# Memory tokens first, two weight parts in buffers of their own, and the second half of x normalised sooner, in a one-core hybrid encoder trunk

## The chip, the cores and the metric

The kernel runs on one core of one Trainium2 chip. The metric is the device time of one execution in microseconds (us), smaller being better. The engines are named as the profile names them: PE is TensorE's matmul side and PEld its weight loads, DVE is VectorE, ACT is ScalarE, POOL is GpSimd, and SP (queue SPq) is the engine that issues every DMA here.

## What is computed

One layer of a streaming encoder, on x of 1024 positions by 1024 features, all in float32:

```
h    = layer_norm(x, ln_in_g, ln_in_b)
proj = h @ w_in + b_in                       # 3912 columns, split among four head groups
ya   = spatial_gating(gelu(a_u), gelu(a_v))  # group A
yb   = chunk_band_attention(bq, bk, bv)      # group B
yc   = dsa_attention(cq, ck, cv, iq, ik, iw) # group C: indexer scores, top 256 keys, attention
km, vm = split(mem @ w_mem_kv, 2)            # 256 memory tokens, 512 columns
ym   = memory_attention(mq, km, vm)          # group M
mixed = concat(ya*silu(a_g), yb*silu(bg), yc*silu(cg), ym*silu(mg))
out  = layer_norm(2**0.25 * h + mixed @ w_out + b_out, ln_g, ln_b)
```

The change lies in the opening: the input norm of x, the product `mem @ w_mem_kv`, and the first columns of `proj` (the indexer's key `ik` and the gate `mg`).

## The kernel before

**Precision.** Every float32 product is made of three passes: each operand is split into a rounded high part and the rest, and high by high, high by rest and rest by high are added up in PSUM (`project`, L211). A block of 128 weight columns is loaded by `wblock` (L193) as a tile `raw` (two buffers, tag `raw`). For each half of its rows ACT writes the high part and POOL subtracts it for the rest (L206, L207). The two halves go into tiles of tag `w`, of which there are five (`WB`).

**The opening, in program order.** `FIRST_LOADS` (L48) gives the order of the first loads: x is a block of 128 rows of x (512 KB), g is the norm's gain broadcast to all partitions, m is half of the memory tokens (512 KB), w is one 128-column block of `w_mem_kv` (512 KB). Then come the norm's shift as columns and the projection's bias (`load_biases`, L145, three loads of single elements by column). `mem_parts` (L319) turns the memory tokens on PE and splits them into `mT` (ACT the high part, DVE the rest). `x_rows` (L289) normalises one block of x: DVE takes the statistics in two pieces, aggregates them, POOL makes the reciprocal root (L133, L134), DVE subtracts and multiplies, ACT scales. `kv_of_mem` (L373) makes the keys (i = 0) and then the values (i = 1) of the memory tokens, 24 matmuls of 256 columns for each of four weight blocks. The third and fourth blocks are loaded inside its first call (L380), into the two `raw` buffers of the first two, so each of these loads waits until POOL has read its predecessor. `x_parts` (L303) turns four normalised blocks of x on PE, 32 transposes for half of the sequence, and splits them into `hTh` (ACT) and `hTl` (DVE). After that come two more weight blocks, `wik` (L388, 72 columns) and `wmg` (L389), again in the `raw` buffers. `ik_half` and `gate_half` (L394, L336) project each half of the sequence with them, 24 matmuls each.

**What holds the second half of x.** Blocks 4 to 7 of x go into tiles of their own tags (`s4`, `score7`, `v3`, `v3`, L284). Two explicit orders stand on them:

```
    with tc.issue_after(loads[3]):
        xts += [x_load(rb) for rb in range(4, NB)]
    ik_half(0, 512)
    with tc.issue_after(first_half[0]):
        for rb in range(4, NB):
            x_rows(rb, xts[rb])
```

The first makes SP issue the four x loads behind the fourth block of `w_mem_kv` (`loads[3]`). The second puts the DVE work of `x_rows` for blocks 4 to 7 behind the last `hTl` of the first half (`first_half[0]` is a DVE instruction).

**Who sets the order.** Each engine runs its instructions in a fixed order. That order is made when the program is built: a planner goes through a simulated time and gives each engine the ready instruction that stands first in the program (some, under `high_priority`, are moved forward). So a change in the opening can move instructions of later stages too. SP serves its DMA issues in its own fixed order. Nearly all operations are recorded under one helper line, L93, so the trace is read by tiles. Behind the opening stand the indexer's queries and scores, the gates of A, then attention groups M, B and C woven with projections and a top-k search on DVE and ACT, then the output projection and the last norm.

Of the kernel before, what the change touches and what calls it, by code (L numbers as in the profile page):

```python
# [11 lines left out]
F32 = mybir.dt.float32  # L12
# [12 lines left out]
P = 128  # L25
NB = 8
KT = 8
# [11 lines left out]

C0_FIRST, LATE = (0, 1, 6, 7, 5), "17 16 15 14 04 13 03 12 02 11 10"  # L40
HR = 2
WH = (0, 0)
MHB = 2
LAG_O = 14
OB, LB = 400, 0
LG_AT = 0
PRELOAD = (6,)
FIRST_LOADS = "xgmxmwxwx"  # L48
ML_V = (6,)
HR_V = 6  # L50
LB_V = (7, 6)
# [21 lines left out]
def f32(ap):  # L73
    return ap.bitcast(F32)
# [3 lines left out]
def tile_trunk(ctx, tc, x, mem, ln_in_g, ln_in_b, w_in, b_in, a_ln_g, a_ln_b, a_ws, a_bs,  # L78
               b_rel_rev, t5_table, w_mem, w_out, b_out, ln_g, ln_b, bucket1h, out):
    nc = tc.nc  # L80
    G, SP = nc.gpsimd, nc.sync
# [22 lines left out]
    def run(steps):  # L104

        while True:
            try:
                next(steps)
            except StopIteration as e:
                return e.value  # L110

    cp = ctx.enter_context(tc.tile_pool(name="cp", bufs=1))
    gp = ctx.enter_context(tc.tile_pool(name="gp", bufs=1))
# [13 lines left out]
    def bcast(t, vec):  # L127
        n = vec.shape[-1]
        SP.dma_start(out=t, in_=bass.AP(tensor=vec.tensor, offset=vec.offset, ap=[[0, P], [1, n]]))
# [39 lines left out]
    def s4(name, dt=F32R, shape=(P, SEQ)):  # L169
        return gp.tile(list(shape), dt, tag="s4", bufs=S4, name=name)  # L170
# [11 lines left out]
    E = ep.enter_context(tc.tile_pool(name="ep", bufs=1))  # L182

    def ev(name, bufs=EV):
        return E.tile([P, 512], F32, tag="ev", bufs=bufs, name=name)
# [4 lines left out]

    loads = []

    def wblock(w, c0, m=P):  # L193

        raw = E.tile([P, KT, P], F32, tag="raw", bufs=2, name="raw")
        loads.append(SP.dma_start(out=raw[:, :, :m], in_=w[:, c0:c0 + m].rearrange("(k p) c -> p k c", p=P)).ins)
        ts = []
        if m < P:
            narrow = [gp.tile([P, 2, KT // 2, m], F32R, tag=tag, bufs=1, name="wnar") for tag in ("planes", "score6")]
        for q in range(2):  # L200
            t = E.tile([P, 2, 4, P], F32R, tag="w", bufs=WB, name="wblk") if m == P else narrow[q]
            r = raw[:, 4 * q:4 * q + 4, :m]
            if WH[0] <= len(loads) < WH[1]:
                G.tensor_scalar(t[:, 0], r, 1.0, 0.0, ALU.mult, ALU.add)
            else:
                S.activation(t[:, 0], r, AF.Copy)  # L206
            G.tensor_sub(t[:, 1], r, f32(t[:, 0]))  # L207
            ts.append(t)
        return ts

    def project(t, a, b, m=P, hi=hh, lo=hl, tag="pp"):  # L211

        acc = bank(tag, "acc")
        for k in range(KT):
            wh, wl = t[k // 4][:, 0, k % 4, :m], t[k // 4][:, 1, k % 4, :m]
            PE.matmul(acc[:m, :b - a], wh, hi(k, a, b), start=(k == 0), stop=False)
            PE.matmul(acc[:m, :b - a], wh, lo(k, a, b), start=False, stop=False)
            PE.matmul(acc[:m, :b - a], wl, hi(k, a, b), start=False, stop=(k == KT - 1))
            yield
        return acc  # L220
# [62 lines left out]
    def x_load(rb):  # L283
        tag = ("S", "S", "S", "S", "s4", "score7", "v3", "v3")[rb]  # L284
        xt = gp.tile([P, DM], F32, tag=tag, bufs={"S": SB, "v3": 2, "s4": S4}.get(tag, 1), name="xt")
        SP.dma_start(out=xt, in_=x[rb * P:(rb + 1) * P, :])
        return xt

    def x_rows(rb, xt):  # L289

        st = E.tile([P, 2, 6], F32, tag="st", bufs=2, name="st")
        V.bn_stats(st[:, 0], xt[:, :512])
        V.bn_stats(st[:, 1], xt[:, 512:])
        mv = E.tile([P, 2], F32, tag="mv", bufs=2, name="mv")
        V.bn_aggr(mv, st)
        rs = E.tile([P, 1], F32, tag="rs", bufs=2, name="rs")
        with tc.high_priority(offset=BOOST):
            rstd_of(mv[:, 1:2], rs)
        V.scalar_tensor_tensor(xt, xt, mv[:, 0:1], g_in, ALU.subtract, ALU.mult)
        with tc.high_priority(offset=BOOST):  # L300
            S.activation(xt, xt, AF.Copy, scale=rs)

    def x_parts(half, xts):  # L303

        high, rest = hT[half]
        for k in range(KT):
            pt = bank(("pt", "qk")[k % 2], "xT")
            for j in range(4):
                PE.transpose(pt[:, j * P:(j + 1) * P], xts[j][:, k * P:(k + 1) * P], ident)
            begin = S.activation(high[:, k, :], pt, AF.Identity, bias=b_col[:, k:k + 1])  # L310
            end = V.scalar_tensor_tensor(rest[:, k, :], pt, b_col[:, k:k + 1], f32(high[:, k, :]), ALU.add, ALU.subtract)
        return end.ins, begin.ins
# [44 lines left out]
    xts, mts, w_kv = [], [], []  # L357
    for what in FIRST_LOADS:
        if what == "x":
            xts.append(x_load(len(xts)))  # L360
        if what == "m":
            mts.append(mem_load(len(mts)))
        if what == "w":
            w_kv.append(wblock(w_mem, len(w_kv) * P))
        if what == "g":
            bcast(g_in, ln_in_g)
# [6 lines left out]
    def kv_of_mem(i):  # L373

        t = ev("kv")
        for pair in range(2):
            acc = run(project(w_kv[2 * i + pair], 0, 256, P, mhi, mlo))
            S.activation(t[:, pair * 256:pair * 256 + 256], acc[:, :256], AF.Copy)
            if not i:
                w_kv.append(wblock(w_mem, 256 + pair * P))  # L380
        return t

    km = kv_of_mem(0)
    first_half = x_parts(0, xts)
    vm = kv_of_mem(1)


    wik = wblock(w_in, I_K, 72)  # L388
    wmg = wblock(w_in, M_G)  # L389
    ikh = s4("ikh")  # L390
# [3 lines left out]
    def ik_half(a, b):  # L394
        acc = run(project(wik, a, b, 72))
        bk = col[I_K]
        with tc.high_priority(offset=BOOST):
            for lo in (0, 64):
                S.activation(ikh[lo:lo + 64, a:b], acc[0:64, :], AF.Identity, bias=bias[0:64, bk:bk + 1])
            S.activation(iwT[64:72, a:b], acc[64:72, :], AF.Identity, bias=bias[64:72, bk:bk + 1])  # L400
            for lo in (0, 64):
                V.scalar_tensor_tensor(ikl[lo:lo + 64, a:b], acc[0:64, :], bias[0:64, bk:bk + 1],
                                       f32(ikh[0:64, a:b]), ALU.add, ALU.subtract)

    with tc.issue_after(loads[3]):
        xts += [x_load(rb) for rb in range(4, NB)]
    ik_half(0, 512)
    with tc.issue_after(first_half[0]):
        for rb in range(4, NB):
            x_rows(rb, xts[rb])  # L410
    run(gate_half(wmg, M_G, 6, 0, "pv"))
    second_half = x_parts(1, xts[4:])
# [375 lines left out]
    for g in range(4):  # L788
        SP.dma_start(out=bsT[64 * (g % 2):64 * (g % 2) + 64, g // 2, :],
                     in_=bass.AP(tensor=a_bs.tensor, offset=a_bs.offset + g * P, ap=[[0, 64], [1, P]]))  # L790
# [438 lines left out]
    def hr_load(rb):  # L1229
        hr = L.tile([P, DM], F32, tag="hr", bufs=HR, name="hr") if rb > HR_S4 else s4("hr", F32)  # L1230
        SP.dma_start(out=hr, in_=h_dram[rb])
        return hr
# [69 lines left out]
    for k in range(KT):  # L1302
        hi, lo = [t[:, k % 4, :] for t in wo[k // 4]]
        raw = E.tile([P, DM], F32, tag="raw", bufs=2, name="rawo")
        SP.dma_start(out=raw, in_=w_out[k * P:(k + 1) * P, :])
        for half in range(2):
            c = slice(half * 512, half * 512 + 512)
# [11 lines left out]
    bcast(bo, b_out)  # L1319
    shift = L.tile([P, DM], F32, tag="hr", bufs=HR, name="shift")  # L1320
    bcast(shift, ln_in_b)
# [59 lines left out]
```

## Time and profile before

| what | value |
|---|---|
| median of 3 runs | 681.34 us (678.85 to 681.65) |
| the profiled execution's own time | 681.43 us |
| its span, first to last instruction | 679.6 us |
| PE busy | 642.8 us, 95% of the span |
| DVE busy | 493.5 us, 73% |
| ACT busy | 421.6 us, 62% |
| POOL busy | 342.2 us, 50% |
| mean granted TensorE clock | 0.984 of full speed |

A busy share is a mean over stages with different limits. PE's 95% says that the time is PE's work and 5% of gaps; what the change can win is in those gaps, and the question is where they lie. Times in the rows are us from the span's start. In brackets behind an instruction stands how long its engine was idle before it, and what released it.

### The profile page before, as it was taken

The numbers are of one execution on the slowest core, as the hardware profiler recorded it, in microseconds if no ns is written. First come the engines' busy times: TensorE is split into PE (matmuls) and PEld (weight loads), VectorE is DVE, ScalarE is ACT, GpSimd is POOL, SyncE is SP. The second block draws the span as 40 slices with busy tenths as digits, with TensorE's granted clock in tenths as the row PEclk, the third lists the DMA queues.
The fourth block names the chain that finished last, engine by engine and source line by source line (L and its number), as shares of the span: only waits on it lengthen the run. The fifth ranks groups of instructions, "written<-read, shape, count | busy, mean of one in ns | idle before, by whom it ended". The sixth has DMA issues, their size and how long they took to land. (4 is left out here: it accounts for less than half of the span.)

```text
span 679.6 us, 11076 instructions
## 1 busy us (share of the span) xinstructions
PE 642.8 (95%) x3698; PEld 486.7 (72%) x3698; DVE 493.5 (73%) x1183; ACT 421.6 (62%) x937; POOL 342.2 (50%) x346
## 2 busy tenths in 40 slices
PE   4889999899999999979999999999998999999995
PEld 3857876677787777757667767667776777777785
DVE  6585256557867899899897888976668688687635
ACT  4665255447599998685898896545545664555310
POOL 3682321105436786483577245983222634559741
PEclk9999999899999999997999999999999999999998
DMA  9793511012234544455467524564102383234111
GB/s 279 235 306 100 169 51 32 1 47 67 73 109 100 108 119 114 90 123 141 82 136 137 101 75 102 115 115 120 35 16 95 126 265 106 89 108 158 63 62 63
DMA packets 121669, 75.30 MB, mean 111 GB/s; under 512 B 58976, under 2 KB 111500, under 8 KB 121612
## 3 DMA queue, kind: packets, MB, share of 16 engines
q1 hardware_dynamic: 121612, 74.59, 40.5%
q8 instruction: 29, 0.48, 0.3%
q14 instruction: 28, 0.23, 0.1%
HBM read 46.44 MB, written 17.64 MB: 94 GB/s over the span
## 5 line engine op out<-in xcount | busy, mean ns | idle before, releaser
L93 PE MATMUL acc<-hTh,wblk 128*128 128x512 f32 (+1 forms) x960 | 322.6, 404 | 4.7 <-DVE iql L93 2.6
L93 PEld LDWEIGHTS acc<-hTh,wblk 128*128 128x128 f32 x960 | 179.0, 191 | 52.8 <-issue 8.2
L93 PE MATMUL acc<-hTl,wblk 128*128 128x512 f32 (+1 forms) x480 | 190.4, 397 | 0.0
L207 POOL TENSOR_TENSOR wblk<-raw,wblk 128x512 fp32r<-128x512 f32 x72 | 101.0, 1407 | 124.3 <-ACT wblk L93 119.0
L93 ACT ACTIVATE jka<-score,cand 128x768 int8<-128x768 f32 (+2 forms) x93 | 96.4, 1037 | 14.8 <-DVE cand L93 14.1
L93 PEld LDWEIGHTS acc<-hTl,wblk 128*128 128x128 f32 x480 | 91.5, 191 | 19.3 <-issue 2.6
L93 PEld LDWEIGHTS <-pT 128*128 128x128 f16 x656 | 45.7, 99 | 32.5 <-issue 25.2
L93 DVE SCALAR_TENSOR_TENSOR score<-relu,iw,score 128x384 f32<-128x384 f32 (+5 forms) x42 | 43.7, 1059 | 23.9 <-ACT relu L93 22.1
L545 POOL TENSOR_TENSOR sc<-sc 128x512 f16<-128x512 f32 (+4 forms) x48 | 58.0, 1213 | 2.3
L93 ACT ACTIVATE wblk<-raw 128x512 fp32r<-128x512 f32 x72 | 44.5, 627 | 23.3 <-PE acc L93 13.5
L93 PE MATMUL acc<-woh,mh 128*128 128x512 f32 (+1 forms) x144 | 55.6, 387 | 0.0
L93 PE MATMUL pv<-v,pT 128*128 128x192 bf16 (+1 forms) x528 | 53.9, 234 | 0.8 <-DMA pT<-sc 0.8
L93 PE MATMUL acc<-wol,mh 128*128 128x512 f32 (+1 forms) x144 | 54.3, 377 | 0.0
L93 PE MATMUL acc<-woh,ml 128*128 128x512 f32 (+1 forms) x144 | 53.7, 374 | 0.4 <-DVE ml L93 0.4
L93 ACT ACTIVATE relu<-qk 128x384 f32<-128x384 f32 (+2 forms) x80 | 35.9, 530 | 24.1 <-PE qk L93 23.7
L544 POOL TENSOR_SCALAR sc<-sc 128x512 f16<-128x512 f32 (+4 forms) x48 | 31.2, 652 | 34.8 <-ACT sc L93 32.8
L93 ACT ACTIVATE sc<-sc,nb 128x640 f32<-128x640 f32 (+7 forms) x64 | 46.5, 729 | 1.4
L93 ACT ACTIVATE pT<-pt 128x512 f16<-128x512 f32 (+3 forms) x48 | 22.3, 484 | 36.1 <-PE pt L93 35.9
L93 DVE TENSOR_SCALAR_CACHE_REDUCE jk<-planes,lo 128x384 bf16<-128x384 uint16 (+2 forms) x48 | 35.7, 744 | 1.2
L93 ACT ACTIVATE o<-o,ri 128x64 f32<-128x64 f32 x96 | 27.9, 340 | 12.4 <-DVE o L93 12.2
L93 PE MATMUL qk<-kh,qh 64*128 64x384 f32 (+3 forms) x96 | 32.7, 417 | 1.9 <-DVE mx L93 1.7
L93 DVE TENSOR_SCALAR_CACHE_REDUCE jk<-planes,cand 128x384 bf16<-128x384 bf16 (+2 forms) x45 | 33.5, 744 | 1.1
(205 smaller groups left out, 1235.1 us busy)
## 6 DMA issues: line engine op xcount, KB each, us to landing
raw<-in_w_in SPq DMA_DIRECT2D x32, 512.0 KB, 3.8
xt<-in_x SPq DMA_DIRECT2D x8, 512.0 KB, 4.8
h_dram<-xt SPq DMA_DIRECT2D x8, 512.0 KB, 5.8
gate<-t SPq DMA_DIRECT2D x16, 256.0 KB, 2.1
rawo<-in_w_out SPq DMA_DIRECT2D x8, 512.0 KB, 4.1
hr<-h_dram SPq DMA_DIRECT2D x8, 512.0 KB, 4.4
out<-hr SPq DMA_DIRECT2D x7, 512.0 KB, 2.6
gate<-gate SPq DMA_DIRECT2D x48, 64.0 KB, 2.0
```

Source lines behind the costliest of these rows:

```text
L93: ins = op(*a, **k)
L207: G.tensor_sub(t[:, 1], r, f32(t[:, 0]))
L544: G.tensor_scalar(high, sc[:, :n], 1.0, 0.0, ALU.mult, ALU.add)
L545: G.tensor_sub(rest, sc[:, :n], high)
```

## The change

The first loads take the order mem, mem, w, x, g, x, w, x, x in place of x, g, mem, x, mem, w, x, w, x. The third and fourth blocks of `w_mem_kv` are loaded outside `kv_of_mem`, each in two halves of 256 KB, into tiles of the tags `jk`, `vt` and `near`, which nothing else uses until much later. The loads of x's blocks 4 to 7 follow them in the program, before the memory's keys, with no order put on them. The DVE work of blocks 4 and 5 is no longer held behind the first half's last `hTl`; that of blocks 6 and 7 still is.

```
+X_FREE = 5
-FIRST_LOADS = "xgmxmwxwx"
+FIRST_LOADS = "mmwxgxwxx"

-    def wblock(w, c0, m=P):
-
-        raw = E.tile([P, KT, P], F32, tag="raw", bufs=2, name="raw")
-        loads.append(SP.dma_start(out=raw[:, :, :m], in_=w[:, c0:c0 + m].rearrange("(k p) c -> p k c", p=P)).ins)
+    def wblock(w, c0, m=P, places=None):
+
+        src = w[:, c0:c0 + m].rearrange("(k p) c -> p k c", p=P)
+        if places:
+            raws = [gp.tile([P, 4, P], F32, tag=tag, bufs=bufs, name="raw") for tag, bufs in places]
+            for q in range(2):
+                loads.append(SP.dma_start(out=raws[q], in_=src[:, 4 * q:4 * q + 4]).ins)
+        else:
+            raw = E.tile([P, KT, P], F32, tag="raw", bufs=2, name="raw")
+            loads.append(SP.dma_start(out=raw[:, :, :m], in_=src).ins)
+            raws = [raw[:, 4 * q:4 * q + 4, :m] for q in range(2)]
...
-            r = raw[:, 4 * q:4 * q + 4, :m]
+            r = raws[q]
...
             acc = run(project(w_kv[2 * i + pair], 0, 256, P, mhi, mlo))
             S.activation(t[:, pair * 256:pair * 256 + 256], acc[:, :256], AF.Copy)
-            if not i:
-                w_kv.append(wblock(w_mem, 256 + pair * P))
         return t
 
+    for pair in range(2):
+        w_kv.append(wblock(w_mem, 256 + pair * P, places=((("jk", 1), ("vt", 1)), (("near", 2), ("near", 2)))[pair]))
+    xts += [x_load(rb) for rb in range(4, NB)]
     km = kv_of_mem(0)
     first_half = x_parts(0, xts)
     vm = kv_of_mem(1)
...
-    with tc.issue_after(loads[3]):
-        xts += [x_load(rb) for rb in range(4, NB)]
     ik_half(0, 512)
-    with tc.issue_after(first_half[0]):
-        for rb in range(4, NB):
+    for rb in range(4, NB):
+        with tc.issue_after(first_half[0]) if rb > X_FREE else ExitStack():
             x_rows(rb, xts[rb])
```

## Rows read from the trace of the kernel before

**Rows 1.** Windows of 40 us: PE, PEld, DVE, ACT, POOL busy, clock, DMA share, GB/s.

```profile
0.00:40.00 40.00, 28.52 (x174) 24.41 (x174) 26.59 (x65) 21.06 (x36) 23.53 (x29) 0.96 0.83 247
40.00:80.00 40.00, 36.43 (x199) 28.59 (x198) 19.85 (x32) 21.97 (x35) 15.02 (x15) 1.00 0.63 209
...
280.00:320.00 40.00, 34.27 (x198) 26.55 (x197) 37.69 (x99) 27.55 (x69) 23.04 (x32) 0.91 0.42 106
```

**Rows 2.** Windows of 5 us in the opening, the same columns.

```profile
10.00:15.00 5.00, 3.42 (x14) 2.25 (x12) 4.96 (x9) 3.84 (x7) 3.08 (x3) 1.00 1.10 383
15.00:20.00 5.00, 4.89 (x29) 4.89 (x29) 4.93 (x10) 1.03 (x2) 5.00 (x6) 0.66 0.86 79
20.00:25.00 5.00, 5.00 (x44) 4.97 (x43) 0.31 (x1) 3.89 (x6) 4.74 (x5) 1.00 0.55 172
...
45.00:50.00 5.00, 2.90 (x23) 2.19 (x21) 2.27 (x4) 3.88 (x6) 1.98 (x4) 1.00 1.02 341
```

**Rows 3.** Timeline of PE in the opening: start, duration, instruction, idle before.

```profile
7.99 1.94 PE L93 MATMUL pt<-ident,mt 128*128 128x128 f32 x8 [7.99 <-DMA mt<-in_mem]
...
17.58 2.39 PE L93 MATMUL acc<-mT,wblk 128*128 128x256 f32 x11
...
22.15 3.16 PE L93 MATMUL acc<-mT,wblk 128*128 128x256 f32 x24
...
33.27 0.46 PE L93 MATMUL acc<-hTh,wnar 128*72 128x512 f32 x1 [1.48 <-ACT wnar L93]
...
44.90 1.25 PE L93 MATMUL xT<-ident,xt 128*128 128x128 f32 x10
...
47.54 0.77 PE L93 MATMUL xT<-ident,xt 128*128 128x128 f32 x5 [1.39 <-ACT xt L93]
```

**Rows 4.** Timeline of SP's DMA issues, from the fourth x block on.

```profile
7.45 2.99 SPq L286 DMA_DIRECT2D xt<-in_x  x1
...
10.96 5.89 SPq L149 DMA_DIRECT2D bias<-in_b_in  x3
...
17.51 4.36 SPq L196 DMA_DIRECT2D raw<-in_w_mem_kv  x2
21.92 2.01 SPq L286 DMA_DIRECT2D xt<-in_x  x4
24.85 10.42 SPq L196 DMA_DIRECT2D raw<-in_w_in  x3
```

**Rows 5.** DMA issues to landing: all x (median), x at 0.72 and 7.45, wik.

```profile
xt<-in_x SPq DMA_DIRECT2D x8, 512.0 KB, 4.8
...
xt<-in_x SPq DMA_DIRECT2D x1, 512.0 KB, 3.4
...
xt<-in_x SPq DMA_DIRECT2D x1, 512.0 KB, 8.6
...
raw<-in_w_in SPq DMA_DIRECT2D x1, 288.0 KB, 7.9
```

**Rows 6.** Timeline of DVE: last row block of the first half, hTl, second half.

```profile
19.02 1.28 DVE L93 SCALAR_TENSOR_TENSOR xt<-xt,mv,g_in 128x1024 f32<-128x1024 f32 x1
27.31 4.04 DVE L93 SCALAR_TENSOR_TENSOR hTl<-xT,b_col,hTh 128x512 fp32r<-128x512 f32 x6 [7.01 <-ACT hTh L93]
...
33.39 2.46 DVE L93 BATCH_NORM_STATS2 st<-xt 128x6 f32<-128x512 f32 x4
...
41.13 4.45 DVE L93 SCALAR_TENSOR_TENSOR xt<-xt,mv,g_in 128x1024 f32<-128x1024 f32 x2
```

**Rows 7.** Timeline of ACT around the first half's high parts.

```profile
25.55 1.15 ACT L93 ACTIVATE wblk<-raw 128x512 fp32r<-128x512 f32 x2 [1.56 <-DMA raw<-in_w_mem_kv]
26.61 2.98 ACT L93 ACTIVATE hTh<-xT,b_col 128x512 fp32r<-128x512 f32 x5
```

**Rows 8.** Instructions on the tile raw to 60 us: ns least, median, most.

```profile
L93 ACT ACTIVATE wblk<-raw x14: 615/620/632, 12.1 to 58.6; 128x512 fp32r<-128x512 f32 x14
L207 POOL TENSOR_TENSOR wblk<-raw,wblk x14: 1277/1296/2342, 13.8 to 59.3; 128x512 fp32r<-128x512 f32 x14
```

## The prediction, made before the changed kernel ran

> **What bounds the kernel now.** I read the busy table first: PE is busy for 642.8 of 679.6 us, so only a gap of PE, or slow clock under PE, can be won. The windows then say where the gaps lie. PE is idle for 11.48 us of the first 40 and 3.57 us of the next 40 [rows 1], which is 15.05 of its 36.8 us of gaps; the stage from 280 to 320 us, far from the change, has another 5.73. In finer windows the opening has two more faces [rows 2]: from 15 to 20 us PE runs at a mean granted clock of 0.66 (a stretch at the lower level, 1.2 GHz), and from 45 to 50 us it is idle for 2.10 us.
>
> The PE timeline names what it waits for [rows 3]. Its first work, the turning of the memory tokens, starts at 7.99 us, released by their DMA. The indexer's key `ik`, the first product that needs x, starts at 33.27, released by ACT's conversion of `wik`. At 44.90 the work on the first half ends and PE turns the second half of x, where it waits for ACT's scaling of late blocks (1.39 us before 47.54).
>
> SP and the DMA views give the cause of 33.27. Two loads of w_mem parts go out in the 4.36 us from 17.51, the second only once POOL has freed a `raw` buffer; the x loads follow at 21.92 and `wik` at 24.85, behind another buffer [rows 4], to land 7.9 us later [rows 5], at 32.75. Meanwhile the DMA engines moved only 172 GB/s from 20 to 25 us, against 383 from 10 to 15 [rows 2]. ACT too stood for 1.56 us for the fourth part, with the first `hTh` queued behind it at 26.61 [rows 7]. DVE ended the first half's rows at 19.02 + 1.28 = 20.30 and then idled 7.01 us [rows 6]. The second half's rows, held behind the last `hTl`, filled it from 33.39 to 41.13 + 4.45 = 45.58, which is 12.2 us for four blocks, 3.05 each.
>
> **The change, part by part.**
>
> *First loads.* The first load of the queue lands 3.4 us after its issue at 0.72 [rows 5]. It is now mem, so PE's first transposes start near 4.1 and not at 7.99. The last of the nine still lands at 7.45 + 8.6 = 16.05, since the bytes are the same. x's first block, first before, is now fourth: at 383 GB/s a load of 0.52 MB takes 1.37 us, so three of them put it near 8.3. DVE then has four blocks, each with two statistics (2.46 us for four), a small aggregate and a multiply of 1.28 [rows 6], which I estimate at 2.8 us; 8.3 + 11.2 is 19.5, so it ends near 20 as before. By itself this buys PE early work and no early x: I count 0 for it, and it is the cover that lets the keys of the first two blocks be over by about 18, where PE was still at them at 22.15 [rows 3].
>
> *Parts three and four, in their own tiles.* The two waits for POOL in SP's queue go. The biases stand ahead as before: SP is busy on them to 10.96 + 5.89 = 16.85 [rows 4], and from 15 to 20 us the DMA engines are 0.86 busy at 79 GB/s [rows 2], so nothing large moves before about 19. From there w_mem parts (1.05 MB), x blocks 4 to 7 (2.10) and `wik` (0.29) are 3.44 MB, 9.0 us at 383 GB/s: `wik` lands between 28 and 29.3. With its ACT conversion PE could start `ik` at 28.8 to 30. Is PE free by then? The fourth part lands near 22 to 23, ACT takes 2 x 0.62, POOL 2 x 1.30 [rows 8], then 24 matmuls of 0.132 (3.16 us for 24) [rows 3]: 23 + 1.2 + 2.6 + 3.2 = 30.0. `hTh` no longer stands behind a late weight on ACT and starts near 22, eight at 0.6 [rows 7], so `hTl` ends near 28. I take `ik` at 30.0: **3.3 us sooner** than 33.27. Bounds: 0, if something else holds it to 33.3, and 4.5 at 28.8. The two extra DMA issues cost SP about 0.4 us each by the spacing of the four x issues (2.01 for four gives 0.5) [rows 4]; the data takes 9 us from 19, so the issues lie under it; uncovered they would cost 1 us.
>
> *Blocks 4 and 5 set free.* They land near 23 to 25 and can fill DVE between and around the `hTl` work (8 x 0.67 us from 4.04 for six [rows 6]). From 22: 5.4 for `hTl`, four blocks at 3.05, 1.5 for `ikl`, is 19.1: the last block leaves DVE near 41 instead of 45.58. PE needs it when its first-half work ends, 44.90 - 3.3 = 41.6, and ACT's scale lies between (1.15 us, as for two weight halves of the same size together [rows 7]), so most of the wait is gone. The gaps of 3.57 us between 40 and 80 us [rows 1] lie mostly here; I take **2.0 us** of them, with bounds 0 and 3.5. SP is passed by these loads too: the stores of x that follow wait for ACT's scaling and only come sooner.
>
> *POOL beside DVE.* More DVE work now lies beside POOL's weight subtraction. These two slow each other: the subtraction took 1.296 us at the median and 2.342 at the most [rows 8], DVE's multiply 1.28 alone and 2.22 each in the pair from 41.13 [rows 6]. One such hit on the path is 1.05; I take **0.5 lost**, bounds 0 and 2.1.
>
> *Clock.* Eleven key matmuls took 2.39 us in the slow stretch and 24 took 3.16 in the fast one [rows 3], 0.217 against 0.132. The stretch from 15 to 20 costs 0.34 x 5 = 1.7 us. It began after PE had worked on and off, with 3.42 of 5 us busy from 10 to 15 [rows 2]. The new opening has such a stretch somewhere as well: 0, bounds -1.7 (it falls where PE waits anyway) and +1.7 (a second one).
>
> *The rest.* The planner orders all engines anew. I see no reason for a sign: 0, with 2 us to either side, since single gaps such as those in the stage at 280 us [rows 1] can grow or shrink by that.
>
> Sum against the profiled execution, 681.43 us (span 679.6 and 1.8 around it, 0.09 over the median of 681.34): 681.43 - 3.3 - 2.0 + 0.5 = 676.6.
>
> **The rivals.** *Slower: x blocks in DVE's way.* Blocks 4 and 5 now may stand ahead of `hTl` in DVE's fixed order. If the planner puts both there and they land as late as before (issue at 21.92 [rows 4], 4.8 at the median [rows 5]), DVE is held to 26.7 + 2 x 3.05 = 32.8, against 27.31 for the first `hTl` now. `hTl` frees the PSUM banks of x's transposes, of which five are there for eight, so three rounds of transposes stay behind it and `ik` starts at about 35.5 (+2.3); blocks 6 and 7 follow `hTl` and give no gain either; a slow-clock stretch adds 1.7: 685.4. It decides if the first `hTl` comes after 29.5. Against it: block 4 should land at 23 to 24, as no buffer holds its load, and then the pair costs only DVE's idle time.
>
> *No change: one term only.* The parts of w_mem wait behind the biases anyway, and ACT must do all of the late blocks, `hTh`, and four conversions between 20 and 30. If this holds `ik` to 32 or later, only 1.3 and half of the second term are left: 681.43 - 1.3 - 1.0 = 679.1. In its favour: ACT was busy for 3.89 of 5 us from 20 to 25 already [rows 2].
>
> *No change: clock.* The mechanism is that PE's new opening is bursts with waits between, and the 48 key matmuls of parts three and four run at the lower level. They would take 48 x 0.085 = 4.1 us more, so `ik` starts at 34.1, 0.8 later than now, and of the rest the second term and POOL's loss remain: 681.43 + 0.8 - 2.0 + 0.5 = 680.7. For it: the stretch at 16 us came after just such gaps. Against it: from 20 us on, the granted clock is 1.00 through gaps of over 2 us at 45 [rows 2]. The Trainium skill has this as a rule (TensorE: Matmul & The Clock Gate, section on HAM oscillation): short bursts between DMA waits fall back to the cold clock again and again. The trace agrees for the burst before 16 us only; by the rule alone the result would be the 680.7 above.
>
> *More.* Both terms at their ends (4.5 and 3.5), with the slow stretch in a wait: 681.43 - 8.0 - 1.7 = 671.7. Each is possible, all three together seldom.
>
> **How the numbers follow.** Half a per cent, 3.4 us, is about what a measurement of this kernel can tell from no change. Forecast 0.55 (674.5 to 679, of which 0.05 lies within half a per cent), more 0.10, one term only 0.17, clock 0.06, slower 0.12. That gives faster 0.60, same 0.28, slower 0.12. The range leaves out the slower case and half of the larger gain, and takes in both cases of no change with some re-ordering: 672 to 682.
>
> **What would show it.** Right: first transposes of mem at about 4 us; w_mem parts three and four issued back to back near 17, then four x loads with no gap; `ik`'s first matmul near 30; x blocks 4 and 5 on DVE before 33; PE idle from 40 to 50 us under 1.5 us; the sum of PE gaps to 80 us about 10 instead of 15. Wrong: `ik` at 33 or later, `hTl` beginning behind a block's statistics after 29.5 us, a second window with a clock near 0.5 before 45 us, or an opening shorter by 5 us with the end not moved, which would put the loss in the planner's order of the later stages.

## The result: 1.3% slower, and the profile after

| | before | after |
|---|---|---|
| median, us (6 runs each) | 681.08 | 689.52 |
| ratio, 95% interval | | 1.0132 [1.0109, 1.0155] |
| profiled execution, us | 681.43 | 689.78 |
| its span, us | 679.6 | 688.0 |
| first indexer matmul `qk` starts, us | 77.14 | 85.75 |

Ratios here and below are estimated from undisturbed runs alone and are not the quotients of the medians, from which they differ by up to 0.18%. The forecast was 676.6 (672 to 682), with 0.12 for slower. The loss is there when the opening ends: the first `qk` matmul starts 8.61 us later, and the span is 8.4 us longer.

The page of the changed kernel, busy time by engine:

```profile
PE 648.0 (94%) x3698; PEld 490.2 (71%) x3698; DVE 491.7 (71%) x1183; ACT 421.8 (61%) x937; POOL 341.1 (50%) x346
```

PE has the same 3698 instructions, but they take 648.0 us instead of 642.8; the other 3.2 us of the longer span are gaps (688.0 - 648.0 = 40.0, against 36.8). Matmuls that take longer without more work point at the clock.

Windows of 40 us after (PE, PEld, DVE, ACT, POOL busy, clock, DMA share, GB/s), to be set beside [rows 1]:

```profile
0.00:40.00 40.00, 27.34 (x154) 23.76 (x155) 24.81 (x61) 22.09 (x35) 23.84 (x30) 0.87 0.76 226
40.00:80.00 40.00, 34.72 (x165) 25.88 (x164) 19.64 (x32) 18.89 (x31) 11.34 (x11) 0.91 0.49 173
280.00:320.00 40.00, 34.48 (x221) 26.94 (x220) 37.18 (x92) 28.07 (x68) 24.62 (x32) 0.91 0.50 112
```

Both opening windows lost on both counts: PE is idle for 12.66 + 5.28 = 17.94 us instead of 15.05, and the clock fell from 0.96 and 1.00 to 0.87 and 0.91. The stage at 280 us stands as it was. Windows of 5 us show where, beside [rows 2]:

```profile
10.00:15.00 5.00, 4.21 (x22) 3.91 (x22) 4.89 (x9) 1.26 (x3) 3.97 (x5) 0.66 1.06 376
15.00:20.00 5.00, 3.40 (x19) 2.96 (x19) 4.74 (x11) 2.48 (x5) 3.97 (x4) 0.84 0.82 67
...
30.00:35.00 5.00, 0.72 (x7) 0.48 (x6) 2.23 (x3) 4.35 (x7) 1.68 (x3) 1.00 0.19 54
35.00:40.00 5.00, 4.96 (x21) 3.50 (x20) 3.80 (x6) 3.96 (x8) 4.15 (x4) 0.66 0.34 62
...
50.00:55.00 5.00, 2.24 (x17) 1.53 (x15) 1.49 (x2) 4.92 (x8) 0.00 (x0) 1.00 0.77 253
55.00:60.00 5.00, 2.99 (x9) 1.93 (x10) 4.89 (x8) 4.68 (x10) 1.95 (x2) 0.60 0.40 150
60.00:65.00 5.00, 5.00 (x20) 3.77 (x19) 2.56 (x5) 0.69 (x1) 0.67 (x1) 0.72 0.01 3
```

From 30 to 35 us PE has next to nothing to do (0.72 of 5), and ACT is the busy engine (4.35). Behind that hole, and again behind the thin stretch from 50 to 60, the clock is at its lower level for a part of the window (of its two levels, 1.2 and 2.4 GHz). Below, "clock loss" is the sum of 5 x (1 - clock) over the sixteen windows to 80 us: 8.5 us after, 1.7 before. It is an upper bound, as a low clock under an idle PE costs nothing.

PE's timeline names the waits, beside [rows 3]:

```profile
4.18 3.65 PE L94 MATMUL pt<-ident,mt 128*128 128x128 f32 x16 [4.18 <-DMA mt<-in_mem]
...
21.08 6.83 PE L94 MATMUL acc<-mT,wblk 128*128 128x256 f32 x48
...
34.63 0.66 PE L94 MATMUL xT<-ident,xt 128*128 128x128 f32 x4 [4.28 <-DVE hTl L94]
35.33 0.60 PE L94 MATMUL acc<-hTh,wnar 128*72 128x512 f32 x1
...
53.80 0.76 PE L94 MATMUL xT<-ident,xt 128*128 128x128 f32 x5 [2.37 <-ACT xt L94]
54.41 0.38 PE L94 MATMUL vt<-ident,kv 128*128 128x128 f32 x2
56.46 0.70 PE L94 MATMUL acc<-hTh,wnar 128*72 128x512 f32 x1 [1.68 <-ACT hTh L94]
```

The memory's products run early, as intended. Then PE stands for 4.28 us before 34.63, and `ik` starts at 35.33 instead of 33.27. The bracket names DVE's `hTl`, but DVE had itself been waiting; one follows the chain back. DVE after, beside [rows 6]:

```profile
19.26 0.31 DVE L94 BATCH_NORM_AGGREGATE mv<-st 128x2 f32<-128x12 f32 x2
19.50 2.48 DVE L94 SCALAR_TENSOR_TENSOR xt<-xt,mv,g_in 128x1024 f32<-128x1024 f32 x2
25.68 1.29 DVE L94 BATCH_NORM_STATS2 st<-xt 128x6 f32<-128x512 f32 x2 [3.70 <-DMA xt<-in_x]
...
29.77 1.28 DVE L94 SCALAR_TENSOR_TENSOR xt<-xt,mv,g_in 128x1024 f32<-128x1024 f32 x1
33.83 2.82 DVE L94 SCALAR_TENSOR_TENSOR hTl<-xT,b_col,hTh 128x512 fp32r<-128x512 f32 x4 [2.77 <-ACT hTh L94]
...
43.23 0.75 DVE L94 SCALAR_TENSOR_TENSOR hTl<-xT,b_col,hTh 128x512 fp32r<-128x512 f32 x1 [3.40 <-ACT hTh L94]
43.90 2.46 DVE L94 BATCH_NORM_STATS2 st<-xt 128x6 f32<-128x512 f32 x4
```

DVE did the rows of blocks 4 and 5 in time (25.68 to 31.05) and then idled 2.77 us for ACT's `hTh`. It idled 3.40 us more for the last `hTh`, so that the rows of blocks 6 and 7, which are held behind the last `hTl`, start only at 43.90. ACT after, beside [rows 7]:

```profile
20.62 0.63 ACT L94 ACTIVATE wblk<-raw 128x512 fp32r<-128x512 f32 x1 [2.86 <-DMA raw<-in_w_mem_kv]
...
24.20 0.63 ACT L94 ACTIVATE wblk<-raw 128x512 fp32r<-128x512 f32 x1 [0.96 <-DMA raw<-in_w_mem_kv]
...
26.54 2.19 ACT L94 ACTIVATE xt<-xt,rs 128x1024 f32<-128x1024 f32 x2 [1.43 <-POOL rs L135]
...
30.07 1.15 ACT L94 ACTIVATE xt<-xt,rs 128x1024 f32<-128x1024 f32 x1 [1.07 <-POOL rs L135]
31.80 1.15 ACT L94 ACTIVATE xt<-xt,rs 128x1024 f32<-128x1024 f32 x1 [0.58 <-POOL rs L135]
...
33.12 1.83 ACT L94 ACTIVATE hTh<-xT,b_col 128x512 fp32r<-128x512 f32 x3
...
41.47 1.15 ACT L94 ACTIVATE wblk<-raw 128x512 fp32r<-128x512 f32 x2 [2.51 <-DMA raw<-in_w_in]
42.53 0.67 ACT L94 ACTIVATE hTh<-xT,b_col 128x512 fp32r<-128x512 f32 x1
```

This is the place. The scales of blocks 4 and 5 (30.07 and 31.80), wanted by PE only past 49, stand ahead of the first `hTh`, which starts at 33.12 instead of 26.61; ACT even waits for the roots that they need. One reason stands in the program: `x_rows` records the roots and ACT's scales under `high_priority`, and `x_parts` records `hTh` without it, so the planner puts a scale that is ready ahead of an `hTh` that the program names sooner. The last `hTh` (42.53) stands behind a weight conversion that waited 2.51 us for its load. Ahead of the scales of blocks 4 and 5 the scales of blocks 2 and 3 run at 26.54, behind the conversions of weight parts three and four. POOL shows why, from 21 us on:

```profile
21.33 1.81 POOL L215 TENSOR_TENSOR wblk<-raw,wblk 128x512 fp32r<-128x512 f32 x1 [2.27 <-ACT wblk L94]
23.10 0.40 POOL L134 TENSOR_SCALAR rs<-mv 128x1 f32<-128x1 f32 x2
23.46 2.53 POOL L215 TENSOR_TENSOR wblk<-raw,wblk 128x512 fp32r<-128x512 f32 x2
25.96 1.07 POOL L135 TENSOR_TENSOR rs<-rs,mhalf 128x1 f32<-128x1 f32 x2
```

DVE had the aggregates of blocks 2 and 3 by 19.6. POOL waited 2.27 us with a subtraction of the third part at its head, whose data was not there, and made the two roots only in the 0.4 us from 23.10 and the 1.07 from 25.96. SP after, beside [rows 4]:

```profile
9.61 7.83 SPq L150 DMA_DIRECT2D bias<-in_b_in  x3
17.49 2.15 SPq L200 DMA_DIRECT2D raw<-in_w_mem_kv  x4
19.68 1.99 SPq L294 DMA_DIRECT2D xt<-in_x  x4
```

The loads do what the change says, one straight behind the other. Nothing is late there.

**The sum of the loss.** `ik` starts 2.06 us later. From 40 to 80 us PE has 5.28 - 3.57 = 1.71 us more gaps. The windows of 35, 55 and 60 us lose 1.7 + 2.0 + 1.4 = 5.1 us to the clock where before there was no loss past 20 us. Together 8.9, against 8.6 at the first `qk`; the 5.1 is the most that the clock can have cost there, since PE was idle for 2.0 us of the second of these windows.

### The profile page after: what moved, and what is told of

The parts are those of the page before. It is cut to its first block, busy times and chain, and to the rows that moved or that the text cites. A ratio compares the mean times of both kernels' runs of the same rounds, so it can differ in the third digit from the quotient of the medians.

```text
span 688.0 us, 11083 instructions
## 1 busy us (share of the span) xinstructions
PE 648.0 (94%) x3698; PEld 490.2 (71%) x3698; DVE 491.7 (71%) x1183; ACT 421.8 (61%) x937; POOL 341.1 (50%) x346
## 4 chain that ended last, share of the span: by engine, by line
PE 62%; DVE 13%; ACT 9%; issue 5%; DMA 5%; POOL 4%; SPq 3%; POOLq 0%; DVEq 0%; ACTq 0%
PE acc L94 44%; PE qk L94 8%; PE pv L94 6%; ACT jka L94 3%; PE pt L94 3%; DVE jk L94 2%; DMA pT<-sc 2%; DMA raw<-in_w_in 2%; SPq L150 1%; DVE vt L94 1%; ACT sc L94 1%; DVE score L94 1%; POOL wblk L215 1%; DVE thr L94 1%; ACT wblk L94 1%
## 5 line engine op out<-in xcount | busy, mean ns | idle before, releaser
L215 POOL TENSOR_TENSOR wblk<-raw,wblk 128x512 fp32r<-128x512 f32 x72 | 98.3, 1370 | 142.2 <-ACT wblk L94 141.1
```

## The experiments

Times in us; `hTh` and `ik` are the starts of the first instruction of each. "Next block" is the start of the first 128x512 product of the weight block that follows the first `qk`. Up to it PE has the same work in every kernel, save the two with fill and a few 8x8 transposes. The first `qk` itself is no such mark: in four kernels (scales held, all rows held, first loads alone, own buffers alone) 24 products of 128x256, which elsewhere stand ahead of it, stand behind it, and it comes some 3.4 us sooner for that alone. The kernel before, run beside each batch, had medians of 681.04 to 681.56.

| kernel | median us | ratio [95%] | first `hTh` | `ik` | next block | clock loss |
|---|---|---|---|---|---|---|
| before | 681.08 | | 26.61 | 33.27 | 77.51 | 1.7 |
| after | 689.52 | 1.0132 [1.0109, 1.0155] | 33.12 | 35.33 | 86.12 | 8.5 |
| scales of blocks 4, 5 held on ACT | 680.92 | 1.0016 [0.9991, 1.0042] | 29.31 | 31.54 | 77.49 | 5.1 |
| own buffers taken out | 679.32 | 0.9976 [0.9954, 0.9997] | 24.14 | 36.67 | 76.22 | 5.1 |
| old first loads | 683.22 | 1.0016 [1.0001, 1.0031] | 27.18 | 33.73 | 80.14 | 5.1 |
| all rows held again | 688.77 | 1.0124 [1.0089, 1.0160] | 30.00 | 32.22 | 84.56 | 5.1 |
| parts 3, 4 behind block 3 | 684.25 | 1.0056 [1.0033, 1.0079] | 26.38 | 34.23 | 80.03 | 3.4 |
| that and scales held | 685.01 | 1.0063 [1.0042, 1.0085] | 26.14 | 34.90 | 80.86 | 5.1 |
| scales held, biases later | 684.20 | 1.0049 [1.0032, 1.0067] | 27.68 | 31.06 | 78.49 | 1.7 |
| 28 matmuls of fill | 686.94 | 1.0080 [1.0052, 1.0107] | 34.79 | 35.52 | 83.77 | 3.4 |
| 28 and 14 of fill | 688.61 | 1.0119 [1.0083, 1.0155] | 33.63 | 34.38 | 87.29 | 5.1 |
| before + first loads | 681.84 | 1.0024 [1.0002, 1.0046] | 28.75 | 32.88 | 78.59 | 5.1 |
| before + own buffers | 680.80 | 0.9999 [0.9982, 1.0016] | 26.82 | 31.95 | 77.56 | 3.4 |
| before + rows of 4, 5 free | 682.63 | 1.0012 [0.9994, 1.0029] | 26.81 | 34.02 | 78.87 | 1.7 |

The last column is rough. With all rows held, the second fill and the biases later, the windows from 10 to 20 us show 1.00 while 22 products of 128x256 in them take 4.26 to 5.06 us; with parts 3 and 4 behind block 3 the same 22 take 2.87. So in these three the column leaves out some 1.4 to 2.2 us, and in the kernel with nothing but the rows of blocks 4 and 5 free about as much (11 in 2.71).

**Two instructions moved back on ACT.** In the changed kernel, the scales of blocks 4 and 5 are put behind the last `hTh` of the first half. Loads, buffers and DVE's freed rows stay.

```
-        with tc.issue_after(first_half[0]) if rb > X_FREE else ExitStack():
+        with tc.issue_after(first_half[0 if rb > X_FREE else 1]):
```

> The changed kernel with only ACT's scales of blocks 4 and 5 put behind the first half's last hTh; DVE still does their rows early. Theory order: hTh near 29.2, ik near 31.5, the second half no later than in the changed kernel; 683 to 686, and faster than with the rows held. Theory first loads: 689 to 690. Theory clock: as the gap before ik shrinks from 4.3 to about 1 us, the slow stretch at 36 goes as well, which is worth 1.7 of it.

ACT of this kernel:

```profile
25.73 2.20 ACT L94 ACTIVATE xt<-xt,rs 128x1024 f32<-128x1024 f32 x2 [1.87 <-POOL rs L135]
...
29.31 1.84 ACT L94 ACTIVATE hTh<-xT,b_col 128x512 fp32r<-128x512 f32 x3
...
35.80 2.18 ACT L94 ACTIVATE xt<-xt,rs 128x1024 f32<-128x1024 f32 x2
...
44.27 2.19 ACT L94 ACTIVATE xt<-xt,rs 128x1024 f32<-128x1024 f32 x2
```

680.92 us, no different from the kernel before: by the ratios the loss falls from 1.32 to 0.16%, some 7.9 us. `hTh` starts 3.8 us sooner, `ik` 3.8, and with the first half's end the scales of blocks 6 and 7 come sooner too (44.27 instead of 49.47 and 52.60). PE's wait of 4.28 us shrinks to 1.29, and of the two behind it (2.37 and 1.68) one is left:

```profile
49.48 0.68 PE L94 MATMUL acc<-hTh,wnar 128*72 128x512 f32 x1 [2.20 <-ACT hTh L94]
```

With equal work behind it PE stands where it stood before the change (77.49 against 77.51): the first `qk`, at 73.68, comes 3.5 us sooner than before only because other products now follow it. The freed rows were harmless on DVE; what they let loose on ACT was not.

**The same rows held again altogether.** The changed kernel with no row freed.

```
-X_FREE = 5
+X_FREE = 3
```

> The changed kernel with the DVE work of all four late x blocks held behind the first half's last hTl again, as before the change. In the changed kernel ACT scaled blocks 4 and 5 at 30.07 and 31.80, ahead of the first hTh at 33.12, and PE idled 4.28 us to 34.63. Theory order (instructions of the late blocks and of the weight parts stand ahead of the first half's chain on ACT and POOL): without these two scales hTh starts near 29.2, right behind block 3's scale (28.73), ik starts near 31.5 instead of 35.33; the second half then comes 2 to 3 us later on DVE. Time 685 to 687. Theory first loads (x now lands too late, everything else follows): no change, 689 to 690. Theory clock (gaps anywhere in the opening cost slow clock): gain only if the slow stretches shrink from 17 us in the first 80.

PE of this kernel, where it turns the second half:

```profile
48.98 0.76 PE L94 MATMUL xT<-ident,xt 128*128 128x128 f32 x5 [2.36 <-ACT xt L94]
...
52.37 1.33 PE L94 MATMUL xT<-ident,xt 128*128 128x128 f32 x5 [2.41 <-ACT xt L94]
```

688.77 us: nearly the whole loss is still there, and it is there by the next block (84.56). `hTh` starts at 30.00, since the conversions of parts three and four still stand ahead of blocks 2 and 3. So the last `hTl`, and all four late blocks behind it, come late; their scales run at 44.65 to 53.93, and PE waits 1.18, 2.36, 2.41 and 1.44 us for them, with a clock of 0.55 and 0.50 from 50 to 60. Freeing the rows alone is therefore not the cause, and holding them is no cure. With these loads and buffers, the rows have to be early and their scales late; the kernels without the own buffers and with the old first loads, below, put scales between the `hTh` and are not slow.

**Weight conversions behind block 3.** In the changed kernel, POOL's subtractions and ACT's conversions of parts three and four are put behind block 3's root and scale. `rstd_of` and `x_rows` return those two instructions.

```
-        w_kv.append(wblock(w_mem, 256 + pair * P, places=...))
+        with tc.issue_after(normed[0]), tc.issue_after(normed[1]):
+            w_kv.append(wblock(w_mem, 256 + pair * P, places=...))
```

> The changed kernel with ACT's and POOL's conversions of w_mem parts three and four put behind block 3's scale and reciprocal root. In the changed kernel the roots of blocks 2 and 3 were ready for POOL at 19.5 and came at 25.96, the scales at 26.54. Theory order: scales near 21 to 22.5, hTh from 24 to 25, ik near 31, since PE does the values' matmuls after that; 677 to 682. Theory first loads: ik not before 33; 686 or more. Theory clock: gaps only move, the slow stretches stay at 13 us or more of the first 80, 684 or more.

PE of this kernel:

```profile
32.47 1.46 PE L94 MATMUL acc<-mT,wblk 128*128 128x256 f32 x10 [0.35 <-POOL wblk L215]
...
34.23 0.48 PE L94 MATMUL acc<-hTh,wnar 128*72 128x512 f32 x1
```

The head of ACT's line is cured (`hTh` at 26.38, as before the change), yet `ik` stands at 34.23 and the time at 684.25, above what I expected. The last ten matmuls of the memory's values now run at 32.47, ahead of `ik`, because POOL subtracts for them last. PE itself waits only 0.35 us there; later it waits 2.37 us before 49.90 and 1.16 before 52.05, for ACT. Of the 2.5 us that it is late at the next block, its gaps to 80 us account for 0.5 (15.54 against 15.05) and the clock for up to 1.7.

**Both cures at once.** The two edits above together.

> The changed kernel with both repairs: ACT's scales of blocks 4 and 5 behind the first half's last hTh, and the conversions of w_mem parts three and four behind block 3's root and scale. With the second alone hTh came early (26.38) but the values' matmuls then ended at 33.9 and ik started at 34.23. Theory order: ik near 33, and no scale of the late blocks in between: 680 to 683, no better than the scales held alone (680.9), since hTh and the weight parts only take each other's place on ACT. If ACT's order of the late blocks were the whole cause of the second repair's loss: 677 to 679.

685.01 us: the cures don't add up, and the expectation was missed. `hTh` starts at 26.14, but the same ten matmuls stand ahead of an `ik` at 34.90, and the next block comes at 80.86, 3.35 later than before the change. To 60 us no wait past 24 us is longer than 1.53, but one stands behind it:

```profile
69.00 0.80 PE L94 MATMUL oh<-oh,tab 32*4 32x384 f32 x2 [2.67 <-ACT wblk L94]
```

This product reads a table, and its bracket names the wrong releaser: SP issued the table's load at 65.85, and it landed at 68.905. Behind this wait the window from 70 to 75 us runs at 0.66. PE's gaps to 80 us are hardly larger than before the change (15.26 against 15.05), while the clock loss is 3.4 larger: by this count nearly all of the 3.35 is the clock's.

**Own buffers taken out.** The changed kernel with parts three and four loaded inside `kv_of_mem` through `raw` again, as before; first loads, early x loads and freed rows stay.

```
+            if not i:
+                w_kv.append(wblock(w_mem, 256 + pair * P))
...
-    for pair in range(2):
-        w_kv.append(wblock(w_mem, 256 + pair * P, places=...))
```

> The changed kernel without the own buffers: parts three and four go through the two raw buffers inside the key product as before; new first loads, early x loads and free rows of blocks 4 and 5 stay. In the fixed orders the roots and scales of blocks 2 and 3 stand ahead of the parts again, but DVE now has the rows of blocks 4 and 5 wholly ahead of the first hTl, and their ACT scales stand between hTh five and six. Theory order: hTh near 24, hTl held by DVE to about 30, ik at 33 to 35; 682 to 687. If the own buffers alone were the cause: 679 to 682.

ACT of this kernel:

```profile
24.14 3.00 ACT L94 ACTIVATE hTh<-xT,b_col 128x512 fp32r<-128x512 f32 x5 [0.42 <-PE xT L94]
27.00 1.17 ACT L94 ACTIVATE wblk<-raw 128x512 fp32r<-128x512 f32 x2
28.04 1.17 ACT L94 ACTIVATE xt<-xt,rs 128x1024 f32<-128x1024 f32 x1
29.08 1.17 ACT L94 ACTIVATE wblk<-raw 128x512 fp32r<-128x512 f32 x2
30.12 1.16 ACT L94 ACTIVATE xt<-xt,rs 128x1024 f32<-128x1024 f32 x1
```

With the weights issued behind the x loads (19.05, against 16.54 for x), nothing stands ahead of blocks 2 and 3: `hTh` starts at 24.14, the late scales follow it, and PE has no wait over 1 us past 28. It pays with a wait of 3.13 us for a weight before 27.71 and `ik` as late as 36.67, yet by 80 us all is made up. At 0.9976 [0.9954, 0.9997] it is the one kernel here whose interval lies below the kernel before, by 0.24%. That is less than the half per cent that I called measurable, and one interval of thirteen that just leaves out 1 is no firm gain.

**Old first loads.** The changed kernel with the old order of the first nine loads.

```
-FIRST_LOADS = "mmwxgxwxx"
+FIRST_LOADS = "xgmxmwxwx"
```

> The changed kernel with the first loads put back in their old order (x, g, mem, x, mem, w, x, w, x); buffers, early x loads and the freed rows stay. In the fixed orders that result, the scale of block 4 stands behind the first five `hTh` on ACT, and the roots of blocks 2 and 3 stand each behind at most a few weight subtractions on POOL. My theory (the loss is ACT's and POOL's order, not the bytes or the number of loads): first `hTh` at 25 to 28 instead of 33.12, `ik` at 31.5 to 33.5 instead of 35.33, no wait of PE over 1.5 us between 45 and 57, half-clock stretches of 3 to 7 us in the first 80 instead of 17.07, and 677.5 to 681.5 in all. Rival A (own buffers with early x loads cost by themselves, since 2.1 MB of x compete with the weights): `ik` at 34.5 or later and 684 to 690. Rival B (the memory tokens first were the one useful part): slower than the changed kernel, above 690.

Ratio 1.0016: most of the loss is gone here as well, with `hTh` at 27.18. The details were missed by a little: `ik` at 33.73, a wait of 2.08 us at 48.91, a clock loss of 5.1 (10 us at the lower level), a median 1.7 us above my upper end. At the next block PE is 2.6 us later than before the change, yet the profiled spans are equal: the time past 80 us is not the same in all these kernels, and why stays open.

**Each part alone, on the kernel before.** Only the new first loads:

> The kernel before with nothing but the new order of the nine first loads. Theory order: the chain of block 3 is not touched, hTh starts between 25 and 27 as before; 679 to 683. Theory first loads: x's first block lands near 9.5 instead of 4.1, hTh and ik are late by about 2 and more; 685 to 689. Theory clock: PE's first work starts at 4.2 with gaps behind it, so slow stretches come earlier and there is a second one: 683 to 685.

Only the own buffers (the x loads are then ordered behind the sixth part load, `loads[5]`, as parts three and four are two loads each):

> The kernel before with nothing but the own buffers: w_mem parts three and four loaded early in two halves each, outside the key and value products; first loads, x's later loads and the rows of blocks 4 to 7 as before. In ACT's order one of block 2's and all of block 3's scaling now stand behind conversions that wait for a DMA. Theory order: block 3's scale near 24 to 25 instead of 22.37, hTh near 26 to 27, ik near 32.5, 681 to 684. Theory clock: no new wait of PE over 1 us in the first 30 us, so no further slow stretch; same range. Against both: 678 or less would show that the early parts are a gain that the rest of the change hides.

Only the rows of blocks 4 and 5 free:

> The kernel before with nothing but the rows of blocks 4 and 5 set free on DVE; the planner puts them between the hTl of the first half, and their ACT scales behind the last hTh. Theory order: nothing stands ahead of the first half's chain, so ik stays near 33.3, and the last block leaves DVE near 41 to 42 instead of 45.58; PE's wait at 46 to 52 shrinks by 1.5 to 2: 678.5 to 680.5, faster than both kernels. Against: 681 or more, if the second half's wait is not what sets the end.

They came to +0.24, -0.01 and +0.12%, of which only the first excludes nought; the third missed its 678.5 to 680.5. In the third, PE's idle time from 40 to 65 us fell from 3.06 to 1.39 as forecast, but a new wait of 1.22 us before 66.98, with a clock of 0.89 and 0.77 from 65 to 75, took the gain back. Their sum, 0.35%, is not the 1.32% of the whole: the loss belongs to the combination. The fourth part of the change, the early x loads, was neither made alone nor taken out. Of the three that were taken out, two cure the loss, the first loads and the own buffers, and each moves blocks 2 and 3 forward again: ACT scales them at 20.88 and 25.02 with the old first loads, and at 20.87 and 22.57 without the own buffers, against 26.54 to 28.73 in the changed kernel.

**The clock by itself.** In the changed kernel, 28 matmuls of 128x256 whose result nobody reads are put behind the memory's values on PE, so that it works through most of the hole before `ik`.

```
+    def fill(n):
+        acc = bank("pv", "fill")
+        PE.after = PE.last
+        for i in range(n):
+            PE.matmul(acc[:, :256], F_W[:, 0, i % 4], mhi(i % 8, 0, 256), start=True, stop=True)
+        PE.after = None
+
+    F_W = w_kv[3][1]
+    fill(28)
```

> The changed kernel with 28 matmuls of 128x256 added on PE behind the last of the memory's keys and values; their PSUM bank is read by nobody, so no result changes. They fill PE's idle 4.28 us before 34.63. ACT and POOL keep their order up to the first hTh (scales of blocks 4 and 5 still ahead of it). Theory order alone (PE only waits): ik still starts at about 35.3, no gain, 689 to 690. Theory clock (the wait itself is only part, the clock that falls behind it is the rest): PE is granted the full clock from 35 to 40 instead of 0.66; the 1.7 us of that stretch come back: 687 to 688.

PE of this kernel, and its windows:

```profile
31.20 3.08 PE L94 MATMUL fill<-mT,wblk 128*128 128x256 f32 x24
35.52 0.45 PE L94 MATMUL acc<-hTh,wnar 128*72 128x512 f32 x1 [1.24 <-ACT hTh L94]
```

```profile
35.00:40.00 5.00, 4.36 (x24) 3.12 (x25) 3.96 (x6) 4.97 (x9) 2.82 (x4) 1.00 0.50 123
...
60.00:65.00 5.00, 5.00 (x28) 3.74 (x27) 2.23 (x5) 1.90 (x3) 0.67 (x1) 1.00 0.00 0
```

`ik` starts no sooner (35.52), and PE has 3.7 us more to do, but 35 to 40 us now runs at 1.00 instead of 0.66 and the kernel ends 2.6 us sooner by the medians (3.5 by the ratios, 1.0132 to 1.0080). PE's gaps to 80 us shrank by only 1.7 us (17.94 to 16.24), so with 3.7 us more work PE would be 2.0 later at the next block at an unchanged clock. It is 2.35 sooner: some 4.3 us come from the clock. A part of that is the window from 60 to 65 us, which the fill does not touch directly. Extra work that shortens a kernel shows the clock's part of the loss apart from the waits.

**A second fill.** The same with 14 unread matmuls of 128x512 more, ahead of the second half's transposes.

> As the one above, with 14 more unread matmuls of 128x512 on PE ahead of the second half's transposes, in the idle stretch from 50 to 54. Theory clock: the slow stretch of 6.8 us at 56 to 63 goes too; with both, up to 1.7 + 3.4 us come back, 684.5 to 686, though the extra work can delay PE by up to 1. Theory order alone: 689 to 691.

688.61 us, inconclusive. The fill missed its hole: PE first waited 4.81 us, and the 14 matmuls ran from 53.23 for 5.26 us, in the way of work that was ready by then.

**Biases out of the way.** The kernel with the scales held, with the three bias loads issued behind the load of `wmg`.

```
-    load_biases()
...
+    with tc.issue_after(loads[-1]):
+        load_biases()
```

> The scales held, and in addition the loads of b_in (7.83 us on SP from 9.61, during which the DMA engines moved 67 GB/s) issued behind wmg's. Parts three and four then go out near 9.6 and land near 17 to 19 instead of 20.6 to 24.2, x blocks 4 to 7 by 24, wik by 25. Theory order: the roots of blocks 2 and 3 no longer wait on POOL for late parts, hTh near 24, ik near 28 to 29; if the second half follows, 676 to 679. If something behind ik sets the end (as when 3.5 us won by the scales held at 77 us were given back): 680 to 682.

Parts three and four were issued from 8.51 us on instead of 17.49, and `ik` came at 31.06, only 0.5 us sooner than with the scales held alone. The time was 684.20, where I had expected 676 to 679: slower than before the change, though the interval overlaps that of the scales held alone. Block 3's scale still waited 2.58 us for its root on POOL, and before 66.62 PE stood for 2.71 us. That was for the same table as with both cures: its load was issued at 63.44 and landed at 66.53, and the windows of 65 and 70 us behind it show 0.75 and 0.91. Earlier bytes gained half a microsecond at `ik`, and a hole of another cause took back more. The expectation took the 3.5 us at the first `qk` for time that had been won; as said above, it was the order of the work.

## Why the prediction was wrong

**The step that failed** stands under the own tiles: "`hTh` no longer stands behind a late weight on ACT and starts near 22". It started at 33.12. Two things were ahead of it: the conversions and subtractions of parts three and four, ahead of the scales and roots of blocks 2 and 3, and the scales of blocks 4 and 5. I asked when each tile's data would be there, and not what stood in front of it in ACT's and POOL's fixed orders once the planner had been given earlier loads. The Trainium skill has the rule (Perfetto Trace Analysis, section on the Tensor Engine Instruction): "ACT/DVE/GPSIMD are strict FIFO." The trace agrees: POOL's 2.27 us at 21.33, with two roots ready behind it.

*First loads, 0.* Alone they measured +0.24%. But "by itself this buys PE early work and no early x" overlooked that it makes the weights' conversions due before x: with the old order of loads in the changed kernel, 1.32% fell to 0.16%. The early work was also counted too fast: the second block's keys were done near 22.5 (an estimate from the 48 products that start at 21.08, which hold keys and values of later blocks too), and DVE ended the rows of block 3 at 21.98 and not near 20.

*Own tiles, 3.3 sooner.* Of the working, the loads held: parts back to back at 17.49, x at 19.68. The fourth part's last conversion ran at 24.20 as reckoned, and the keys and values were done by 30. `ik` came 2.06 us later instead. With the own buffers as the only change `ik` comes at 31.95, 1.3 sooner, and the time is the same (0.9999): the size of the first term in the case called "one term only".

*Blocks 4 and 5 free, 2.0.* DVE did its part before 33 as forecast, and PE had no idle time from 40 to 50; the gap only moved, as the first half ended at 49.57 instead of 44.90. Alone, this part won 1.7 us of idle time between 40 and 65 us, near the 2.0, and none of it reached the end. The step looked at DVE, and of ACT's scale only at its 1.15 us, not at where it would stand.

*POOL beside DVE, 0.5.* No run tried it by itself. The multiplies of blocks 6 and 7 were not hit: they took 2.43 us after, 4.45 before [rows 6]. A hit of about the priced size fell elsewhere, as POOL's subtraction at 21.33 took 1.81 us, beside DVE's multiplies of blocks 2 and 3, where 1.28 is usual, and the two roots stand behind it.

*Clock, 0 with 1.7 to either side.* Mis-sized: up to 5.1 us more in the windows past 30; with the fill some 4.3 at equal work came back. The weighing took the granted clock of 1.00 through gaps of over 2 us as evidence against. Those were the idle time of a whole window (2.10 of 5 us), and the longest single wait in it was 1.39; the new hole was 4.28 us, and from 30 to 35 us PE worked for 0.72 us. The rule of the Trainium skill that I cited (TensorE: Matmul & The Clock Gate, HAM oscillation) was right as to its kind, here with waits for DVE and ACT in place of DMA: behind each thin stretch a window shows 0.60 to 0.72.

*The slower rival* had the right shape and the wrong engine. It put blocks 4 and 5 in the way of `hTl` on DVE, with its deciding point at 29.5 for the first `hTl`. That came at 33.83 and `ik` at 35.33 (forecast there: 35.5), but they were in the way on ACT, so that the right time there was luck. With one slow stretch it came to 685.4; the two further ones make up to 3.4 of the remaining 4 us, an estimate from their windows. Its chance of 0.12 rested on one engine, while three carry each block.

## What to carry to other kernels

Where a planner fixes each engine's order, moving a load earlier moves every instruction that hangs on it forward on its engine, perhaps ahead of something that is wanted sooner; so for each freed instruction ask, on every engine that it touches, what stands behind it. Price a new hole in PE's work by the hole and by the slow clock behind it: here the waits cost 2.06 + 1.71 us and the slow clock up to 5.1. When parts that cost little alone cost 1.3% together, take one out at a time from the whole rather than adding one at a time to the old kernel.

## What the runs showed of the hardware that I had not expected

- Filling a hole with 3.7 us of unread matmuls made the kernel 2.6 us faster (686.94 against 689.52).
- The three bias loads, 15 KB in all, hold SP's queue for 5.89 us before and 7.83 us after, and from 15 to 20 us the DMA engines are 0.82 busy at 67 GB/s. Yet moving them out of the way won 0.5 us at `ik` and nothing in the time.
- POOL's tiny root steps take longer beside DVE's multiply: after, the second step (128x1) took 1.45 us at 28.58, beside a multiply that ran from 28.35 to 29.63, and 0.55 at 31.21, when the next multiply was over (31.05).
- A late `ik` need not make a kernel slow: with the own buffers taken out, `ik` starts 3.4 us later than before the change, `hTh` 2.5 us sooner, and the kernel is no slower (0.9976).
